# A hybrid decoder layer: the relative-bias product moved to the third value slice and done in one fp32r pass

## The chip, the cores and the metric

The kernel runs on one core of a Trainium2 chip. The metric is the device time of one execution in microseconds (us). Before the change the median of three runs is 200.31 us (199.53 to 201.07).

## The reference

One layer on x of 256 x 1024, float32. One projection `h = x @ w_in` gives queries, keys and values of two attention branches, their gates z, and two branch gates:

```python
ya = swa_sink_attention(qa, ka, va, sinks, table_a) * silu(za) @ w_out_a
yb = moba_attention(qb, kb, vb, table_b) * silu(zb) @ w_out_b
merged = sigmoid(ga + b_gate[:D]) * ya + sigmoid(gb + b_gate[D:]) * yb
x = layer_norm(alpha * x + merged @ w_out, gamma, beta)
```

Branch A has 8 query heads on 2 key heads, a window of 128 and one sink logit per head; branch B has 8 heads and, at 256 positions, one causal block. To the logits of every head a bias is added that depends on the distance of query and key: `rel_table[t5_bucket(distance), head]`, a table of 32 buckets by 16 heads.

## The kernel before, in words

**Numbers.** Most products are made of three fp32r products: an operand is split into a high part (rounded to fp32r by ScalarE, ACT) and the rest (a subtraction on VectorE, DVE), and high x high, high x low and low x high are summed. So each weight tile that SyncE (SP) loads is rounded by ACT (L138) and subtracted by DVE (L153) before TensorE (PE) uses it. The bias product (L312) is a plain fp32 product instead.

**Order.** The schedule is written by hand: each engine runs its instructions in the order of the program. `order` (L93 to L105) lists the weight pieces: eight value slices `v`, then the tiles `t` of keys, queries, gates, with the bias reads `r` put between them (one after each query tile), then `a`, `b` and `o`. `lead` (L167) runs `fetch` (load and rounding) some pieces ahead of the use and `split` (subtraction) one piece less ahead: at value slice k the fetch of slice k+2 and the split of slice k+1 are issued, and only then the products of slice k. A raw buffer serves five pieces (`RAWS`), so a load waits until the subtraction five pieces earlier is done.

**Value stage** (L302 to L318): for k = 0 to 7, twelve products of 320 columns each (L307) into four banks.

**Bias.** At k = 0 the value loop also makes, for two sets of heads, the product of the table with a one-hot matrix (L312), copies it reversed into `rvec` on DVE (L313) and writes `rvec` to the DRAM tensor `rd` by GpSimd (POOL) (L314). `fetch("r", n)` (L120) reads it back with a shifted row step, so that each partition gets its own diagonal: `toep`. SP's queue holds these reads in its fixed order: t0, t1, two reads of `rd`, t2, two reads, t3, and so on. The first read waits for the first write of `rd`. POOL also issues the small loads (L72 to L77: table, one-hot, sinks, gate bias), and after them builds the identity and `eps`.

**First projections.** `keys(KA, 0)` (L334) multiplies t0; in ACT's order the rounding of t2 comes before its copies of that product (L196). DVE (L198) and POOL (L200) then build `kall`; `queries` (L202) with t1 and t2 builds `q` (L206 to L212, POOL last). `scores` (L224 to L241) multiplies `q` by `kall`, adds `toep` (L226, L239) and takes exponentials. Twelve steps of this (L335) run through all heads, then gates, output and norm.

Of the kernel before, what the change touches and what calls it, by code (L numbers as in the profile page):

```python
# [11 lines left out]
F32 = mybir.dt.float32  # L12
F32R = mybir.dt.float32r
BF16 = mybir.dt.bfloat16
AF = mybir.ActivationFunctionType
ALU = mybir.AluOpType

P = 128
# [4 lines left out]
NB = 32  # L23
# [5 lines left out]
RL = 384  # L29
# [17 lines left out]
def hybrid_layer(ctx: ExitStack, tc: tile.TileContext, xT, x2, w_t, w_v, w_a, w_b, w_o,  # L47
                 b_gate, sinks, table, onehot, gamma, beta, out):
    nc = tc.nc
    const = ctx.enter_context(tc.tile_pool(name="const", bufs=1))  # L50
    wp = ctx.enter_context(tc.tile_pool(name="wp", bufs=1))
    work = ctx.enter_context(tc.tile_pool(name="work", bufs=2))
# [6 lines left out]
    def bank(tag):  # L59
        return psum.tile([P, 512], F32, tag=tag, name=f"ps_{tag}", bufs=banks[tag])  # L60
# [6 lines left out]

    rvec = work.tile([P, 2, RL], F32, tag="pr_", name="rvec", bufs=4)
    nc.gpsimd.memset(rvec, NEG)
    tab = const.tile([NB, 2 * P], F32, name="tab")  # L70
    oh = work.tile([NB, RL], F32, tag="res", name="oh")
    nc.gpsimd.dma_start(tab, table)  # L72
    nc.gpsimd.dma_start(oh, onehot)
    sink = const.tile([P, 8], F32, name="sink")
    nc.gpsimd.dma_start(sink, sinks)
    bg = const.tile([P, 16], F32, name="bg")
    nc.gpsimd.dma_start(bg, b_gate)  # L77
    ident = const.tile([P, P], F32, name="ident")
    make_identity(nc, ident)
    nsink = const.tile([P, 8], F32, name="nsink")  # L80
    eps = const.tile([P, 1], F32, name="eps")
    nc.gpsimd.memset(eps, LN_EPS)


    kall = const.tile([P, 3, 2, 2, S], F32R, tag="big12", name="kall")
# [87 lines left out]
    def weights(kind, n):  # L173
        lead(kind, n)
        return ready[kind, n]
# [126 lines left out]
    for k in range(NK):  # L302
        wh, wl = weights("v", k)
        for a, w, s0, s1 in ((xh, wh, k == 0, False), (xl, wh, False, False), (xh, wl, False, k == NK - 1)):
            for c in range(2):
                for t in range(2):
                    nc.tensor.matmul(vacc[t][c], a[:, k, t * P:(t + 1) * P], w[:, c * 320:(c + 1) * 320],  # L307
                                     start=s0, stop=s1)
        if k == 0:
            for s, (lo, hi) in enumerate(REACH):  # L310
                pr = bank("pt")[:, :hi - lo]
                nc.tensor.matmul(pr, tab[:, s * P:(s + 1) * P], oh[:, s * P:s * P + hi - lo], start=True, stop=True)  # L312
                nc.vector.tensor_copy(rvec[:, s, TOP + 1 - hi:TOP + 1 - lo], pr[:, ::-1])  # L313
                nc.gpsimd.dma_start(rd[s].rearrange("(p l) -> p l", p=P), rvec[:, s, :])  # L314
            nc.gpsimd.tensor_scalar_mul(nsink, sink, -1.0)
# [46 lines left out]
    for br, (tiles, w_y) in enumerate(((GA, "a"), (GB, "b"))):  # L362
        for c in range(8):
# [9 lines left out]
            else:  # L373
                m = work.tile([P, S], F32, name="m")
# [27 lines left out]
    for t in range(2):  # L402
        ts = slice(t * P, (t + 1) * P)
        res = work.tile([P, D], F32, tag="res", name="res")
# [129 lines left out]
```

## Time and profile before

| | us |
|---|---|
| median of 3 runs | 200.31 |
| the profiled execution | 199.98 |
| its span (first to last instruction) | 198.2 |
| PE busy in it | 189.4 |
| DVE, ACT, POOL busy | 135.5, 113.8, 47.8 |

PE is the TensorE matmul, PEld its weight loads. A group of instructions is named by its line in the kernel, its engine and "out<-in". "issue to landing" of a transfer counts from its issue until its data is there. Busy matmuls are pipelined, so each lasts longer than its distance to the next.

### The profile page before, as it was taken

The numbers are of one execution on the slowest core, as the hardware profiler recorded it, in microseconds if no ns is written. First come the engines' busy times: TensorE is split into PE (matmuls) and PEld (weight loads), VectorE is DVE, ScalarE is ACT, GpSimd is POOL, SyncE is SP. The second block draws the span as 40 slices with busy tenths as digits, with TensorE's granted clock in tenths as the row PEclk, the third lists the DMA queues.
The fourth block names the chain that finished last, engine by engine and source line by source line (L and its number), as shares of the span: only waits on it lengthen the run. The fifth ranks groups of instructions, "written<-read, shape, count | busy, mean of one in ns | idle before, by whom it ended". The sixth has DMA issues, their size and how long they took to land.

```text
span 198.2 us, 3922 instructions
## 1 busy us (share of the span) xinstructions
PE 189.4 (96%) x1469; PEld 177.9 (90%) x1469; DVE 135.5 (68%) x274; ACT 113.8 (57%) x228; POOL 47.8 (24%) x92
## 2 busy tenths in 40 slices
PE   8999999999999999999999999999999999999970
PEld 3799999799999999889999999999999999888860
DVE  0686277987797794586769537446685878785863
ACT  4675756578867867875669454245554746630211
POOL 7110083467699673020000000000000000003311
PEclk9999999999999999999999999999999999999998
DMA  5999999834453543054656885564847499300202
GB/s 131 300 401 364 286 322 302 264 121 159 136 187 109 174 146 111 0 160 161 211 173 203 314 246 157 185 212 140 286 146 244 158 342 341 154 0 0 106 0 106
DMA packets 14082, 37.43 MB, mean 189 GB/s; under 512 B 1632, under 2 KB 5744, under 8 KB 14064
## 3 DMA queue, kind: packets, MB, share of 16 engines
q1 hardware_dynamic: 13520, 36.51, 56.6%
q0 software_dynamic: 256, 0.49, 0.7%
q8 instruction: 11, 0.18, 0.4%
q10 hardware_dynamic: 288, 0.20, 0.3%
q14 instruction: 7, 0.06, 0.1%
HBM read 35.75 MB, written 1.44 MB: 188 GB/s over the span
## 4 chain that ended last, share of the span: by engine, by line
PE 73%; DMA 9%; DVE 5%; ACT 5%; POOL 3%; issue 2%; SPq 1%; DVEq 0%; ACTq 0%; POOLq 0%
PE ps_acc L181 18%; PE ps_acc L182 18%; PE ps_acc L184 18%; PE ps_acc L412 6%; DMA wraw<-in_w_v 5%; PE ps_sc L412 4%; DMA wraw<-in_w_t 3%; PE ps_pt L272 2%; PE ps_o L289 2%; PE ps_pt L412 1%; ACT wh L138 1%; PE ps_sc L232 1%; DVE wl L153 1%; PE ps_sc L224 1%; ACT pr__1159 L241 1%
## 5 line engine op out<-in xcount | busy, mean ns | idle before, releaser
L181 PE MATMUL ps_acc<-xh,wh 128*128 128x256 f32 x296 | 71.7, 281 | 0.0
L182 PE MATMUL ps_acc<-xl,wh 128*128 128x256 f32 x296 | 71.4, 280 | 0.0
L153 DVE TENSOR_TENSOR wl<-wraw,wh 128x1024 fp32r<-128x1024 f32 (+1 forms) x53 | 61.2, 1169 | 6.6 <-ACT wh L138 6.3
L138 ACT ACTIVATE wh<-wraw 128x1024 fp32r<-128x1024 f32 (+2 forms) x54 | 52.7, 989 | 8.4 <-DMA wraw<-in_w_v 4.1
L181 PEld LDWEIGHTS ps_acc<-xh,wh 128*128 128x128 f32 x296 | 55.8, 189 | 0.2 <-issue 0.2
L182 PEld LDWEIGHTS ps_acc<-xl,wh 128*128 128x128 f32 x296 | 55.8, 188 | 0.0
L184 PE MATMUL ps_acc<-xh,wl 128*128 128x256 f32 x296 | 40.9, 280 | 0.0
L184 PEld LDWEIGHTS ps_acc<-xh,wl 128*128 128x128 f32 x296 | 37.5, 189 | 0.0
L400 POOL CAST wh<-sums 128x2 fp32r<-128x2 f32 x8 | 1.4, 180 | 92.3 <-ACT sums L396 92.3
L367 ACT ACTIVATE sg<-ps_acc,bg 128x256 f32<-128x256 f32 x16 | 7.6, 474 | 19.1 <-PE ps_acc L184 19.1
L181 PE MATMUL ps_acc<-yh,wh 128*128 128x256 f32 x64 | 15.8, 281 | 0.0
L182 PE MATMUL ps_acc<-yl,wh 128*128 128x256 f32 x64 | 15.8, 280 | 0.0
L200 POOL CAST kall<-kall 64x512 fp32r<-64x512 f32 x10 | 10.7, 1066 | 15.0 <-DVE kall L198 14.5
L372 DVE TENSOR_TENSOR ga<-ps_acc,sg 128x256 f32<-128x256 f32 x8 | 3.4, 424 | 13.7 <-ACT wh L138 13.7
L181 PEld LDWEIGHTS ps_acc<-yh,wh 128*128 128x128 f32 x64 | 12.1, 188 | 0.0
L182 PEld LDWEIGHTS ps_acc<-yl,wh 128*128 128x128 f32 x64 | 12.0, 188 | 0.0
L184 PE MATMUL ps_acc<-yh,wl 128*128 128x256 f32 x64 | 10.1, 279 | 0.0
L377 ACT ACTIVATE mm<-m 128x256 fp32r<-128x256 f32 x8 | 3.3, 418 | 11.6 <-DVE m L376 11.6
L150 DVE TENSOR_TENSOR wl<-wraw,wh 128x1024 fp32r<-128x1024 f32 x8 | 9.7, 1218 | 0.1
L198 DVE TENSOR_TENSOR kall<-ps_acc,kall 64x256 fp32r<-64x256 f32 x10 | 4.2, 422 | 7.8 <-ACT kall L196 7.6
L412 PE MATMUL ps_acc<-wh,mm 128*128 128x512 f32 x32 | 8.8, 396 | 0.0
L184 PEld LDWEIGHTS ps_acc<-yh,wl 128*128 128x128 f32 x64 | 8.6, 188 | 0.0
(170 smaller groups left out, 306.5 us busy)
## 6 DMA issues: line engine op xcount, KB each, us to landing
wraw<-in_w_t SPq DMA_DIRECT2D x37, 512.0 KB, 4.1
wraw<-in_w_o SPq DMA_DIRECT2D x8, 512.0 KB, 4.9
wraw<-in_w_v SPq DMA_DIRECT2D x7, 320.0 KB, 5.4
toep<-rd SPq DMA_DIRECT2D x16, 128.0 KB, 6.5
wraw<-in_w_a SPq DMA_DIRECT2D x4, 512.0 KB, 3.2
wraw<-in_w_b SPq DMA_DIRECT2D x4, 512.0 KB, 3.9
xraw<-in_xT SPq DMA_DIRECT2D x8, 128.0 KB, 5.2
xr<-in_x SPq DMA_DIRECT2D x1, 1024.0 KB, 7.4
```

The costliest lines, as they stand in the source:

```text
L138: nc.scalar.activation(wh[:, cut], raw[:, cut], AF.Copy)
L150: nc.vector.tensor_sub(quarters(wl), raw.rearrange("p (a b) -> p a b", a=4), quarters(wh).bitcast(F32))
L153: nc.vector.tensor_sub(wl[:, :width], raw[:, :width], wh[:, :width].bitcast(F32))
L181: nc.tensor.matmul(acc, wh[:, cols[k]], ah[:, a0 + k, :], start=(k == 0), stop=False)
L182: nc.tensor.matmul(acc, wh[:, cols[k]], al[:, a0 + k, :], start=False, stop=False)
L184: nc.tensor.matmul(acc, wl[:, cols[k]], ah[:, a0 + k, :], start=False, stop=(k == n - 1))
L198: nc.vector.tensor_sub(l[r, j, :], acc[r, :], h[r, j, :].bitcast(F32))
L200: nc.gpsimd.tensor_copy(kall[halves[1 - j], b, :, j, :], kall[r, b, :, j, :])
L272: nc.tensor.transpose(pt[:, b * P:(b + 1) * P], pr[:, j, b * P:(b + 1) * P], ident)
L289: nc.tensor.matmul(o[r, :], vv[:, 0, c], pts[:, :S], start=True, stop=False)
L367: nc.scalar.activation(sg, acc, AF.Sigmoid, bias=bg[:, at:at + 1])
L412: nc.tensor.matmul(acc, a[:, k, ts], w[:, q:q + n, :cols], start=s0, stop=s1)
```

## The change

The small loads are issued after the identity and `eps`. The table and the one-hot are loaded twice each, on partitions 0 to 31 and 32 to 63, and POOL casts the one-hot to fp32r (`places`). At the end of k = 1 ACT rounds the table to fp32r on all 64 rows (`parts`), and DVE replaces the lower 32 rows by the rest. At the end of k = 2 one fp32r product over 64 rows takes the place of the fp32 product of k = 0; the copies and the writes to `rd` follow it there.

```diff
--- before.py
+++ after.py
@@ -67,19 +67,24 @@
 
     rvec = work.tile([P, 2, RL], F32, tag="pr_", name="rvec", bufs=4)
     nc.gpsimd.memset(rvec, NEG)
-    tab = const.tile([NB, 2 * P], F32, name="tab")
-    oh = work.tile([NB, RL], F32, tag="res", name="oh")
-    nc.gpsimd.dma_start(tab, table)
-    nc.gpsimd.dma_start(oh, onehot)
-    sink = const.tile([P, 8], F32, name="sink")
-    nc.gpsimd.dma_start(sink, sinks)
-    bg = const.tile([P, 16], F32, name="bg")
-    nc.gpsimd.dma_start(bg, b_gate)
     ident = const.tile([P, P], F32, name="ident")
     make_identity(nc, ident)
     nsink = const.tile([P, 8], F32, name="nsink")
     eps = const.tile([P, 1], F32, name="eps")
     nc.gpsimd.memset(eps, LN_EPS)
+
+    rows = [slice(i * NB, (i + 1) * NB) for i in range(2)]
+    tab = const.tile([2 * NB, 2 * P], F32, name="tab")
+    oh = work.tile([2 * NB, RL], F32, tag="res", name="oh")
+    for r in rows:
+        nc.gpsimd.dma_start(tab[r, :], table)
+        nc.gpsimd.dma_start(oh[r, :], onehot)
+    sink = const.tile([P, 8], F32, name="sink")
+    nc.gpsimd.dma_start(sink, sinks)
+    bg = const.tile([P, 16], F32, name="bg")
+    nc.gpsimd.dma_start(bg, b_gate)
+    places = work.tile([2 * NB, RL], F32R, tag="pts", name="places", bufs=4)
+    nc.gpsimd.tensor_copy(places, oh)
 
 
     kall = const.tile([P, 3, 2, 2, S], F32R, tag="big12", name="kall")
@@ -306,10 +311,14 @@
                 for t in range(2):
                     nc.tensor.matmul(vacc[t][c], a[:, k, t * P:(t + 1) * P], w[:, c * 320:(c + 1) * 320],
                                      start=s0, stop=s1)
-        if k == 0:
+        if k == 1:
+            parts = work.tile([2 * NB, 2 * P], F32R, tag="m", name="parts")
+            nc.scalar.activation(parts, tab, AF.Copy)
+            nc.vector.tensor_sub(parts[rows[1], :], tab[rows[1], :], parts[rows[1], :].bitcast(F32))
+        if k == 2:
             for s, (lo, hi) in enumerate(REACH):
                 pr = bank("pt")[:, :hi - lo]
-                nc.tensor.matmul(pr, tab[:, s * P:(s + 1) * P], oh[:, s * P:s * P + hi - lo], start=True, stop=True)
+                nc.tensor.matmul(pr, parts[:, s * P:(s + 1) * P], places[:, s * P:s * P + hi - lo], start=True, stop=True)
                 nc.vector.tensor_copy(rvec[:, s, TOP + 1 - hi:TOP + 1 - lo], pr[:, ::-1])
                 nc.gpsimd.dma_start(rd[s].rearrange("(p l) -> p l", p=P), rvec[:, s, :])
             nc.gpsimd.tensor_scalar_mul(nsink, sink, -1.0)
```

## Rows read from the trace of the kernel before

**Rows 1.** The page: busy time, and the granted clock in 40 slices.
```profile
PE 189.4 (96%) x1469; PEld 177.9 (90%) x1469; DVE 135.5 (68%) x274; ACT 113.8 (57%) x228; POOL 47.8 (24%) x92
...
PEclk9999999999999999999999999999999999999998
```

**Rows 2.** Waits of PE: line, who released it, us in total, times, longest.
```profile
PE ps_sc L224 <- POOL q L212: 0.5, 1, 0.5
PE ps_sc L224 <- DVE nm L239: 0.5, 1, 0.5
...
PE ps_pt L272 <- POOL pr__1159 L264: 0.4, 1, 0.4
```

**Rows 3.** The chain of waits, 16 to 31 us: start, us, what.
```profile
16.01 6.66 DMA wraw<-in_w_t
...
22.75 1.06 ACT wh L138
23.81 0.34 ACT kall L196
...
27.37 0.39 POOL q L211
...
27.83 1.28 POOL q L212
...
30.07 0.40 PE ps_sc L224
...
30.50 0.43 DVE low L226
```

**Rows 4.** Timeline of SP's queue, 11 to 17 us: start, us, instruction.
```profile
11.88 1.54 SPq L133 DMA_DIRECT2D wraw<-in_w_t  x2
14.67 1.25 SPq L120 DMA_DIRECT2D toep<-rd  x2
16.01 0.54 SPq L133 DMA_DIRECT2D wraw<-in_w_t  x1
```

**Rows 5.** Waits of SP's queue.
```profile
SPq L120 <- DMA rd<-rvec: 1.2, 1, 1.2
```

**Rows 6.** Timeline of PE: the bias product, and the first products of slices 1 and 3.
```profile
7.47 0.92 PE L312 MATMUL ps_pt<-oh,tab 32*128 32x128 f32 x4
...
8.31 0.19 PEld L307 LDWEIGHTS ps_acc<-wh,xh 128*128 128x128 f32 x1 [0.33 <-ACT xh L124]
...
11.80 0.19 PEld L307 LDWEIGHTS ps_acc<-wh,xh 128*128 128x128 f32 x1
```

**Rows 7.** Timeline of DVE, 8 to 12 us.
```profile
8.71 0.61 DVE L313 COPY rvec<-ps_pt 128x128 f32<-128x128 f32 x2
...
10.31 0.42 DVE L146 TENSOR_TENSOR xl<-xraw,xh 128x256 fp32r<-128x256 f32 x1
11.02 0.83 DVE L153 TENSOR_TENSOR wl<-wraw,wh 128x640 fp32r<-128x640 f32 x1 [0.29 <-ACT wh L138]
```

**Rows 8.** Timeline of ACT: the rounding of slices 1 and 3.
```profile
7.20 0.74 ACT L138 ACTIVATE wh<-wraw 128x640 fp32r<-128x640 f32 x1 [0.69 <-DMA wraw<-in_w_v]
...
10.25 0.74 ACT L138 ACTIVATE wh<-wraw 128x640 fp32r<-128x640 f32 x1 [0.43 <-DMA wraw<-in_w_v]
```

**Rows 9.** Timeline of POOL: its first load, the writes of the bias.
```profile
1.40 0.73 POOL L72 DMA_DIRECT2D tab<-in_table  x1
...
9.29 1.11 POOL L314 DMA_DIRECT2D rd<-rvec  x2 [4.93 <-DVE rvec L313]
```

**Rows 10.** DMA issues: count, KB, us to landing; the tile is the one issued at 33.91.
```profile
rd<-rvec POOLq DMA_DIRECT2D x2, 192.0 KB, 5.5
...
wraw<-in_w_t SPq DMA_DIRECT2D x1, 512.0 KB, 4.4
...
wraw<-in_w_a SPq DMA_DIRECT2D x4, 512.0 KB, 3.2
```

**Rows 11.** DMA queues, first 9 us: packets, MB, share of 16 engines' time.
```profile
q0 software_dynamic: 128, 0.09, 5.2%
```

## The prediction

> **What bounds the kernel now.** Read the page's busy shares first: TensorE (PE) is busy 96% of the span, its clock is full except at the very end [rows 1]. Then ask where PE waits at all: after the first slices it waits three times, 1.4 us together [rows 2]. So the kernel is a PE stream, and a change can pay only by taking work out of that stream or one of those waits, and can cost by making a wait longer. The longest two stand at the scores, L224; the chain of waits says what ends the first one, at 30.07 us [rows 3]: the third key/query weight tile (call it t2, the second query tile) is issued at 16.01, lands 6.66 us later, is rounded by ScalarE (ACT) at 22.75, and only then, because ACT works in order, ACT copies the key product (L196); VectorE (DVE) and GpSimd (POOL) build the key and query operands, and PE gets the second query half at 30.07. The third view is SyncE's queue (SP): t2's issue stands behind the first two toep reads, and these wait for the bias rows to land in DRAM [rows 4], 1.2 us already now [rows 5]. So the bias product, tiny on PE, is the head of a chain that ends in a PE wait. That is what the change moves.
>
> **The change part by part.** The sums are made against the profiled execution, 199.98 us (span 198.2 and 1.8 around it); the median of the three runs is 200.31, so 0.33 is added at the end.
>
> *The product leaves value slice k=0.* Now two fp32 products (four matmul records) run from 7.47, and the next slice starts behind them at 8.31 [rows 6]. Its weights were rounded by 7.20+0.74 = 7.94 [rows 8]. Without the product it can start at about 7.98: a gain of 0.33 us, not of the 0.84 us that the product takes, since the rest lay in a wait for ACT. DVE also loses 0.61 us of copies there [rows 7].
>
> *Small loads later, six for four.* The identity and eps go first; the first load issue moves from 1.40 to about 2.1. With at most 0.73 us each [rows 9] the second copy of the one-hot is issued by about 4.5; with the 5.5 us that the slower POOL transfers took [rows 10] it lands by 10.0. Nothing needs it before the new place of the product (11.4, below). I cost it at nothing; the cover is 1.4 us, less the cast that follows.
>
> *The cast of the one-hot on POOL (64x384).* Nearest are the 64x256 casts: 0.39 us in the open and 1.28 us beside a DVE subtraction [rows 3], so 0.6 to 1.9 for one and a half times the width. I take 0.6 to 1: done by about 11, just in time. At 1.9 it is done at 11.9, which is no later than the DVE step it is joined with. Skill sentence: "GPSIMD Engine Reference", Key points, in the Trainium skill, says that GpSimd shares its SBUF interfaces with VectorE and contends with two-input DVE instructions; the two durations just given agree, and by that rule the cast would come out near 1.9, by the open row near 0.6; the sum is the same either way.
>
> *Table parts (ACT copy 64x256, DVE subtraction 32x256) at k=1.* In ACT's order the copy comes after the rounding of slice 3's weights, which ends at 10.25+0.74 = 10.99 [rows 8]. The key copy on 64 partitions took 0.34 to its release [rows 3], so the copy ends at about 11.37. The DVE subtraction (0.42 as for 256 columns [rows 7]) is placed behind slice 2's and ahead of slice 3's, so it runs 11.41 to 11.8, and slice 3's xl and wl, which began at 10.31 and 11.02 [rows 7], follow it: xl to 12.1, wl to about 12.9.
>
> *The product at k=2.* Two slices take 11.80-8.31 = 3.49 us [rows 6]; from 7.98, PE is through slice 2 at 11.47, and waits for the parts until 11.85: +0.38. The new products are 384 columns; the bounds are 0.84 us (as the fp32 pair now) and, at the pace of the stream (slice: 12 products of 320 columns in 1.75 us), 384/320 x 0.146 = 0.18. I take 0.3, nearest to the stream's fp32r rows, as the short product may not run at the full pace. Slice 3 so starts at about 12.15 instead of 11.80: PE +0.35 net, the 0.33 gained at the front included. Slice 3's wl is wanted two thirds into the slice, at 13.3, and is there at 12.9: no further wait.
>
> *What goes on from there.* The two copies (L313) stand in DVE's order behind slice 3's wl: they start at about 12.85 instead of 8.71, and the first write to DRAM is issued 9.29-8.71 = 0.58 after that, at 13.4 instead of 9.29 [rows 7, 9]: +4.1 us. It lands 5.4 to 5.5 later [rows 10], about 18.8, against 14.67 now. SP's order is fixed: the two weight tiles t0 and t1 go out earlier (each a microsecond or so later than now, since their buffers come free with slice 3's and 4's wl; they are wanted after slice 7), then SP sits on the first toep read, and behind it wait t2, two more toep reads, t3 and so on. The two reads cost 1.34 us up to t2's issue [rows 4], so t2 is issued at about 20.15.
>
> *Its landing.* Now 6.66 us, into a full queue. After the hold SP has had nothing to issue for about 4 us, and the queue is nearly drained. Bounds: 3.2 us (the median of the branch weights, same size) and 6.66; the nearest row is a tile issued into a short queue, 4.4 us [rows 10]. So t2 lands at 24.5, 1.9 us later than now; and if the DRAM write, too, is a little faster in a thinner queue (5.1), 1.6 us later. I take 1.6. By the bounds it is 0.7 to 4.1. t3 follows t2 through the same queue at the same distance, so it sets nothing by itself.
>
> *What hides and what does not.* Every step between t2's landing and 30.07 is back to back [rows 3], so PE gets its operands at 31.7. PE itself comes to that point 0.35 later than now, so its wait grows from 0.5 by 1.6 less 0.35, to about 1.8 us, and all the small gains and losses on PE before it (0.33, 0.38, 0.3) vanish in it. After 30.07 PE is the bound again nearly without gaps [rows 2], and the first toep rows, read at 19 to 20, are not used before 30.5 [rows 3]: the 1.6 us stay. 199.98 + 1.6 + 0.33 = 201.9 us.
>
> **The rivals.** *Hidden after all.* If the DRAM write and t2 land as fast as the fastest rows (3.2 each), the first toep read goes at 16.6, t2 at 17.95, and it lands at 21.2, before 22.67: then the key copy waits for PE alone, 0.2 to 0.35 later: 200.5 us. For it: the queue is thinner. Against it: the writes took 5.5 us, and t0 and t1 are in flight with them.
>
> *Faster.* One mechanism: slice 1 starts 0.33 earlier, and the parts are ready early enough (no wait at 11.47), with the hold on SP so short that t2 is not late. Then the operands come at the old time or up to the 0.5 of the wait earlier, and the gain is at most 0.33+0.5 = 0.83: 199.5 us. It decides from t2's issue: at 16.0 or before. Against it: DVE's order alone puts the DRAM write 3 us or more later. A gain over 1% (2.0 us) is more than those three waits and the 0.33 hold (1.7), so it is all but excluded.
>
> *Worse.* The added loads delay the value weights of slice 3. The software queue's packets took 5.2% of all engines' time in the first 9 us [rows 11], 0.47 us; the doubled table and one-hot can add as much again. Slice 3's rounding, the parts, wl, the write and t2 then all come 0.3 to 0.5 later, and t2's landing is nearer to 6.66 than to 4.4, say 5.7, if the toep reads ahead of it fill the queue as they do now: 1.6 + 0.4 + 1.3 = 3.3: 203.6 us. Skill sentence: "DMA: Bandwidth & Descriptors", Issuing engines are not separate DMA queues, in the Trainium skill, says that transfers issued from GpSimd and SyncE run on the same 16 engines and interleave; by that rule the extra loads do slow the weights, and the share in rows 11 bears it out in kind. A clock that falls in a wait of nearly 2 us would be dearer still, but in rows 1 it falls only at the end, with PE idle.
>
> *Not what it says.* If the fp32r products are no quicker than the fp32 pair (0.84), PE comes to 30.07 another 0.5 late: still inside the wait, no change to the sum.
>
> **How the numbers follow.** Forecast (t2 late by 0.8 to 2.6 us: 201.1 to 202.9) 0.47; hidden 0.25; faster 0.10; worse 0.18. The range that leaves out most of the faster case and the far end of the worse one is 200.0 to 203.7. About 1% (2.0 us) is what a measurement here can tell from no change. Slower by over 1%: two fifths of the forecast case and nearly all of the worse one, 0.36. Faster by over 1%: 0.04. Within: 0.60.
>
> **What would show it.** Right: slice 1's first product near 8.0; a PE wait of about 0.4 ahead of L312 at k=2; the DRAM write issued near 13.4; SP waiting for it 4 us or more at L120 (1.2 now); t2 issued near 20; PE waiting over 1.5 us at L224. Wrong: t2 issued before 18, or a chain to the first scores that no longer runs through t2; or PE gaps of their own in slices 3 to 7.

## The result, and the profile after

The changed kernel takes 202.45 us (median of 4 runs, 202.35 to 203.16) against 200.49 for the kernel before in the same comparison: ratio 1.0112, 95% interval 1.0082 to 1.0142. It is slower by about 2 us, inside the range and on the side that was forecast (201.9). In the sections below "before" is 200.24 to 200.28 us, the medians of the larger comparisons that the experiments ran in. The profiled execution of the changed kernel took 203.16 us, span 201.4; its line numbers are five higher than before up to the value loop, and those of the kernels below differ by a few more.

The waits of PE in the changed kernel (line, who released it, us in total, times, longest):

```profile
PE ps_sc L229 <- POOL q L217: 1.6, 2, 1.1
PE ps_acc L312 <- ACT wh L143: 1.3, 1, 1.3
...
PE ps_pt L321 <- DVE parts L317: 0.4, 1, 0.4
```

The wait at the first scores was 0.5 [rows 2] and is now 1.6; the wait for the parts is new. The 1.3 at L312 is the gap ahead of value slice 1, which the fp32 product used to fill [rows 6].

The chain of waits of the changed kernel, 13 to 33 us (start, us, what), beside [rows 3]:

```profile
13.29 0.29 DVE rvec L322
...
13.87 4.76 DMA rd<-rvec
18.64 0.62 SPq L125
...
19.99 5.35 DMA wraw<-in_w_t
25.42 1.06 ACT wh L143
26.48 0.27 ACT kall L201
...
28.41 1.50 POOL kall L205
...
30.43 1.28 POOL q L217
...
32.68 0.57 PE ps_sc L229
```

The chain now starts at the bias copies and runs through the DRAM write and the first toep read into t2, as was forecast. t2 is rounded at 25.42 instead of 22.75, 2.67 us later, and the first scores' second half comes at 32.68 instead of 30.07, 2.61 later: nothing between the two gave.

What the small parts did stands in the timelines of the changed kernel (start, us, instruction, idle before it and who ended it), first PE:

```profile
8.16 0.42 PE L312 MATMUL ps_acc<-wh,xh 128*128 128x320 f32 x1 [1.28 <-ACT wh L143]
...
12.32 0.46 PE L321 MATMUL ps_pt<-places,parts 64*128 64x128 f32 x2 [0.38 <-DVE parts L317]
12.71 0.42 PE L312 MATMUL ps_acc<-wh,xh 128*128 128x320 f32 x1
```

then ACT:

```profile
7.37 0.74 ACT L143 ACTIVATE wh<-wraw 128x640 fp32r<-128x640 f32 x1 [1.16 <-DMA wraw<-in_w_v]
...
10.68 0.74 ACT L143 ACTIVATE wh<-wraw 128x640 fp32r<-128x640 f32 x1 [0.65 <-DMA wraw<-in_w_v]
11.33 0.40 ACT L316 ACTIVATE parts<-tab 64x256 fp32r<-64x256 f32 x1
```

DVE:

```profile
11.76 0.41 DVE L317 TENSOR_TENSOR parts<-tab,parts 32x256 fp32r<-32x256 f32 x1 [1.30 <-ACT parts L316]
...
12.55 0.82 DVE L158 TENSOR_TENSOR wl<-wraw,wh 128x640 fp32r<-128x640 f32 x1
13.29 0.61 DVE L322 COPY rvec<-ps_pt 128x128 f32<-128x128 f32 x2
```

POOL:

```profile
9.16 0.51 POOL L87 CAST places<-oh 64x384 fp32r<-64x384 f32 x1 [3.87 <-DMA oh<-in_onehot]
13.87 1.08 POOL L323 DMA_DIRECT2D rd<-rvec  x2 [4.20 <-DVE rvec L322]
```

and SP's queue:

```profile
13.43 1.89 SPq L138 DMA_DIRECT2D wraw<-in_w_t  x2
18.64 1.25 SPq L125 DMA_DIRECT2D toep<-rd  x2
19.99 0.94 SPq L138 DMA_DIRECT2D wraw<-in_w_t  x1
```

Slice 1 starts at 8.16 (8.31 before): little is gained, because its weights were rounded only by 7.37+0.74 = 8.11. The cast is done at 9.67, far ahead of the parts, so the parts alone set the product: 0.38 us of waiting, then 12.71-12.32 = 0.39 for the two fp32r products. Slice 3's first product is at 12.71. In the kernel before it was at 11.94, 0.77 us earlier; the 11.80 in [rows 6] is the load of its weights, which runs ahead of it:

```profile
11.94 0.31 PE L307 MATMUL ps_acc<-wh,xh 128*128 128x320 f32 x1
```

One thing more is in this execution. Its busy shares by microsecond (us, PE busy, PEld, DVE, ACT, POOL, granted clock, DMA share, GB/s):

```profile
31.00:32.00 1.00, 0.24 (x1) 0.19 (x1) 0.44 (x1) 0.76 (x1) 0.94 (x2) 1.00 0.98 315
32.00:33.00 1.00, 0.46 (x2) 0.32 (x2) 0.40 (x1) 0.57 (x2) 0.88 (x3) 0.86 1.03 410
33.00:34.00 1.00, 1.00 (x6) 1.00 (x6) 0.59 (x3) 0.00 (x0) 0.88 (x3) 0.50 1.11 293
...
37.00:38.00 1.00, 1.00 (x11) 1.00 (x10) 0.80 (x1) 1.00 (x2) 0.00 (x0) 1.00 1.03 301
```

After the two waits PE ran at 0.50 of full speed, the 1.2 GHz level, for some 3 us (0.50 in each of the three from 33 to 36): 6 products in a full us, against 11 once the clock is back at 2.4 GHz. "TensorE: Matmul & The Clock Gate", Part 1, in the Trainium skill, says that the clock has these two levels and follows how busy the array has lately been; these rows agree.

### The profile page after: what moved, and what is told of

Read it like the earlier page. It is cut to its first block, busy times and chain, and to the rows that moved or that the text cites. A ratio compares the mean times of both kernels' runs of the same rounds, so it can differ in the third digit from the quotient of the medians.

```text
span 201.4 us, 3923 instructions
## 1 busy us (share of the span) xinstructions
PE 190.5 (95%) x1467; PEld 179.6 (89%) x1467; DVE 135.6 (67%) x275; ACT 113.9 (57%) x229; POOL 49.3 (25%) x95
## 4 chain that ended last, share of the span: by engine, by line
PE 76%; DMA 8%; DVE 3%; ACT 3%; POOL 3%; SPq 2%; issue 2%; DVEq 0%; ACTq 0%; POOLq 0%
PE ps_acc L186 19%; PE ps_acc L187 19%; PE ps_acc L189 19%; PE ps_acc L421 6%; PE ps_sc L421 4%; DMA wraw<-in_w_v 3%; PE ps_pt L277 3%; DMA wraw<-in_w_t 3%; DMA rd<-rvec 2%; PE ps_sc L237 2%; PE ps_o L294 2%; PE ps_pt L421 1%; PE ps_sc L229 1%; ACT pr__1166 L246 1%; POOL kall L205 1%
## 5 line engine op out<-in xcount | busy, mean ns | idle before, releaser
L186 PE MATMUL ps_acc<-xh,wh 128*128 128x256 f32 x296 | 72.8, 284 | 0.0
L187 PE MATMUL ps_acc<-xl,wh 128*128 128x256 f32 x296 | 72.4, 283 | 0.0
L186 PEld LDWEIGHTS ps_acc<-xh,wh 128*128 128x128 f32 x296 | 56.7, 191 | 0.2 <-issue 0.2
L187 PEld LDWEIGHTS ps_acc<-xl,wh 128*128 128x128 f32 x296 | 56.5, 191 | 0.0
```

Of the source, the lines that this page charges most:

```text
L186: nc.tensor.matmul(acc, wh[:, cols[k]], ah[:, a0 + k, :], start=(k == 0), stop=False)
L187: nc.tensor.matmul(acc, wh[:, cols[k]], al[:, a0 + k, :], start=False, stop=False)
```

## The experiments

The theory to test, called the hold: the late DRAM write holds SP's queue, t2 comes late behind it, and PE waits at the first scores. Its rival, called the front: the time is lost in the value stage, to loads, parts and product.

**The move alone.** The kernel before with only the place of the product changed:

```diff
-        if k == 0:
+        if k == 2:
             for s, (lo, hi) in enumerate(REACH):
```

> The kernel before, with the fp32 bias product, its copies and writes moved from k=0 to k=2 and nothing else. Theory of the hold (the late DRAM write holds SyncE's queue, so t2 comes late and TensorE waits at the first scores): the copies stand behind slice 3's subtraction, about 11.8, the write goes out about 12.3 (9.29 before, 13.87 after), t2 is issued about 18.7 (16.01 and 19.99), the first scores come about 1.5 us later than before: 201.5 to 202.0 us. Rival (the front: the loss is what TensorE loses in the value stage to loads, parts and product): the product of 0.84 us now stands in the dense stream and 0.33 is gained at k=0, 0.5 in all: 200.9 to 201.1 us.

Measured: 200.87 us, ratio 1.0046 (1.0023 to 1.0069). The hold's 201.5 to 202.0 failed. SP does wait for the write (first read at 16.92, write at 12.96, t2 at 18.27), but t2 then landed in 4.2 us instead of 6.66, so it is rounded no later than before (22.58, and 22.75 before), and in ACT's timeline the key copy waits for PE, not for t2's rounding:

```profile
22.58 1.09 ACT L138 ACTIVATE wh<-wraw 128x1024 fp32r<-128x1024 f32 x1
24.56 0.78 ACT L196 ACTIVATE kall<-ps_acc 64x256 fp32r<-64x256 f32 x2 [0.89 <-PE ps_acc L184]
```

So with PE 0.8 us later, a t2 issued at 18.27 and landing in 4.2 us has no cost of its own. The 0.6 us are the rival's: the fp32 product of 0.84 us now stands in the dense stream, and the first scores come 0.81 later (30.88). The rival's 200.9 to 201.1 is missed by 0.03.

**The loads alone.** The kernel before with its four small loads moved behind the constants:

```diff
-    nc.gpsimd.dma_start(tab, table)
...
     nc.gpsimd.memset(eps, LN_EPS)
+    nc.gpsimd.dma_start(tab, table)
```

> The kernel before, with its four small loads issued after the identity and eps; product at k=0. Hold theory: the one-hot lands by about 7.5, just when the product starts (7.47), so the write moves by 0.3 us at most, and t2 with it: 200.3 to 200.8 us. Rival (the later small loads slow the value weights): slice 1's weights land 0.2 later as in the changed kernel and TensorE keeps that loss: 200.7 to 201.0 us, with t2's issue unmoved.

Measured: 200.43 us, ratio 1.0000 (0.9979 to 1.0021); t2's issue at 16.01, as before. Later loads cost nothing that this interval can tell.

**The reads one tile later.** This is the deciding run: the changed kernel, with t2 ahead of the first reads in SP's order.

```diff
+    held = []
     for t in range(GA):
-        order += [("t", t)]
+        order += [("t", t)] + held
+        held = []
         if QA <= t < KQB:
-            order.append(("r", t - QA))
+            held = [("r", t - QA)]
...
```

> The changed kernel, with each pair of toep reads put one weight tile later in SyncE's order, so that t2 goes ahead of the first reads. Hold theory: t2 is issued when its buffer comes free, about 16 (19.99 in the changed kernel), lands by 21.5, the key copy waits for TensorE alone (its key tile ends about 24.5), the first scores come about 30.8 to 31.2, the clock stays up, 200.6 to 201.3 us: half or more of the loss is gone though the bias and the loads stay where the change put them. Rival (the front): nothing of this matters, 202.2 to 202.6 us.

Measured: 201.00 us, ratio 1.0041 (1.0021 to 1.0060). With the bias, loads and parts where the change put them, 202.45-201.00 = 1.45 us of the loss are gone (1.4 by the two ratios, each to the kernel before in its own comparison). Its SP queue, with t2 the third of the tiles at the first row:

```profile
13.73 2.96 SPq L140 DMA_DIRECT2D wraw<-in_w_t  x3
17.97 1.26 SPq L127 DMA_DIRECT2D toep<-rd  x2
```

and its key copy is released by PE:

```profile
24.97 0.78 ACT L203 ACTIVATE kall<-ps_acc 64x256 fp32r<-64x256 f32 x2 [0.92 <-PE ps_acc L191]
```

The 201.00-200.24 = 0.76 us above the kernel before that stay are the front's.

**The control**, the same shift in the kernel before:

> The kernel before with the same shift of the reads, the control. Hold theory: t2 is issued about 14.4 instead of 16.01, but the key tile ends at 23.62 and the key copy starts at 23.77 already, so at most 0.2 us: 200.1 to 200.5 us. If the shift by itself were worth a microsecond or more (its own effect, not the hold's), 199.0 to 199.5 us.

Measured: 200.07 us, ratio 0.9992 (0.9976 to 1.0007). By itself the shift is worth 0.2 us by the medians, and nothing that the interval can tell, so the 1.45 us, or all but 0.2 of them, are the hold's.

**A larger dose.** The changed kernel with parts at k=2 and product at k=3:

```diff
-        if k == 1:
+        if k == 2:
             parts = work.tile([2 * NB, 2 * P], F32R, tag="m", name="parts")
...
-        if k == 2:
+        if k == 3:
             for s, (lo, hi) in enumerate(REACH):
```

> The changed kernel with everything of the bias one slice later: parts at k=2, product, copies and writes at k=3; SyncE's order as in the changed kernel. Theory of the hold: the parts are ready when the product comes, so TensorE loses no 0.38 us there, but the write goes out about 1.0 to 1.7 us later than 13.87, t2 is issued about 21 to 21.7, and the first scores come 1 us or more after 32.68: 203.0 to 204.5 us. Rival (the front): without the wait for the parts TensorE gains 0.4: 201.9 to 202.2 us.

Measured: 203.83 us, ratio 1.0188 (1.0151 to 1.0225). PE no longer waits for parts, yet the kernel is slower still, as the hold says and the front denies. SP's queue, PE at the first scores, and the chain of waits ahead of them:

```profile
19.81 1.45 SPq L125 DMA_DIRECT2D toep<-rd  x2
21.36 0.54 SPq L138 DMA_DIRECT2D wraw<-in_w_t  x1
```

```profile
33.24 0.38 PE L229 MATMUL ps_sc<-kall,q 128*128 128x256 f32 x1 [1.86 <-POOL q L217]
34.16 0.38 PE L229 MATMUL ps_sc<-kall,q 128*128 128x256 f32 x1 [0.54 <-POOL q L217]
```

```profile
23.21 6.58 DMA wraw<-in_w_t
...
29.87 1.06 ACT wh L143
```

The tile in this chain is not t2 but t3, which stands behind the next two reads in the same queue: its rounding comes ahead of the query copy in ACT's order. So here t3 sets the first scores, which the prediction had left out ("it sets nothing by itself").

**Both**, product at k=3 and the reads one tile later:

> The same, with the reads one tile later in SyncE's order as in the third run. Hold theory: t2 is ahead of the hold, so what is left is the front alone; with the parts ready, TensorE pays the product (0.39) and what slice 1's weights come late: 200.4 to 200.9 us, less than the 201.00 of the product at k=2 with the reads later. If the write's delay still counted by another way (t3 behind the reads, or the bias late for the scores), 201.5 us or more.

Measured: 201.26 us, ratio 1.0053 (1.0033 to 1.0073). The write is the latest of all (15.77) and costs nothing more that the intervals can tell (201.00 had 1.0021 to 1.0060), so the bias itself is not late for the scores. But it is not better than the 201.00 with the product at k=2, as the wait for the parts that it avoids should have made it: that part of the expectation failed. In its profiled execution slice 1 began only at 9.34, for weights that landed late.

**What the front is made of.** Two runs more on the 0.76 us: the changed kernel with the reads later and all six loads ahead of the constants, and the kernel before with the reads later and the six loads, the second copies unused.

```diff
     nc.gpsimd.memset(rvec, NEG)
-    ident = const.tile([P, P], F32, name="ident")
-    make_identity(nc, ident)
...
     nc.gpsimd.dma_start(bg, b_gate)
+    ident = const.tile([P, P], F32, name="ident")
+    make_identity(nc, ident)
...
```

> The changed kernel with the reads one tile later (third run) and its six small loads issued ahead of the constants again. It splits the 0.8 us that the third run left, the front. If the place of the loads is part of the front (slice 1 starts late because the value weights land late), slice 1 starts at 8.0 to 8.2 and the time is 200.4 to 200.8 us; if the front is the wait for the parts and the product in the stream (0.2 to 0.4 and 0.39), nothing moves: 200.9 to 201.2 us.

Measured: 201.10 us, ratio 1.0035 (1.0012 to 1.0058).

```diff
-    nc.gpsimd.dma_start(tab, table)
-    nc.gpsimd.dma_start(oh, onehot)
...
+    for r in rows:
+        nc.gpsimd.dma_start(tab[r, :], table)
+        nc.gpsimd.dma_start(oh[r, :], onehot)
...
```

> The kernel before with the reads one tile later, and of the change the loads alone: table and one-hot loaded twice, all six loads after the constants; the fp32 product at k=0 uses the first copy, the second is read by nothing. If the doubled loads delay the value weights by the 0.3 to 0.5 us that the software queue's share allows, 200.4 to 200.7 us; if they hide, as 200.07 of the same kernel with four loads: 200.0 to 200.2 us.

Measured: 200.30 us, ratio 1.0005 (0.9983 to 1.0026). The place of the loads is not the front. For their number the run falls between its two expectations: 0.23 us above the same kernel with four loads (200.07), which the two intervals cannot tell from nothing; that a part of the 0.76 is theirs is neither shown nor excluded. Seen in the traces are the product in the stream (0.39 us in the changed kernel) and the wait for the parts (0.38). How the 0.76 divides is not settled, since the run without that wait (product at k=3) was no faster.

**The clock.** Four products of constants on PE ahead of the first scores, their result unused:

```diff
+        if i == 1:
+            warm = bank("o")
+            for _ in range(4):
+                nc.tensor.matmul(warm, nc.const_aps.tensor(1.0, [P, P], BF16), ...)
```

> The changed kernel with four products of constants (128x512, bf16) on TensorE just ahead of the first scores, where it waited 1.06 us; their result is not used. If the waits of 1.06 and 0.54 us are what let the clock fall after 32.8 us, it stays at 2.4 GHz, and the time is 0.3 to 1 us less than the changed kernel's: 201.4 to 202.1 us. If the fall costs nothing in the median, or is not due to the wait: 202.3 to 202.7 us.

Measured: 202.32 us, ratio 1.0115 (1.0073 to 1.0157), no change. The waits shrank to 0.34 and 0.54 and the clock stayed up in the profiled execution, but in it the operands also came earlier (second half at 32.09, against 32.68; the tile that set them was t3, as with the product at k=3), so it does not isolate the clock. And the changed kernel once more:

> The changed kernel itself, timed in the same call as its variants: 202.2 to 202.7 us. The look at the trace is for the clock: if the fall after the first scores belongs to every execution it is there again; if it depends on how long the waits happen to be, t2's landing differs with it.

Measured: 202.67 us, ratio 1.0113 (1.0072 to 1.0153). Here the waits were 0.92 and 0.54, and the clock stayed up: 202.56 us in the profiled execution. So the fall belongs to some executions: the 203.16 of the first profile holds it, the 202.56 of the second does not, and as the medians (202.45 and 202.67) lie near the second, the 2 us do not need it.

**A version that beats both?** With t2 free of the hold, DVE can subtract it, and t3, while it is idle, ahead of the key parts and not beside POOL's casts. First t2 alone, then both, in the kernel before with the reads later (shown for both; for t2 alone the step is taken at ("t", 0) only):

```diff
-        advance(1, at, far - 1)
+        advance(1, at, far - ((kind, n) not in (("t", 0), ("t", 1))))
```

> The kernel before with the reads one tile later and with VectorE's subtraction for t2 issued ahead of the key parts, while VectorE is idle, so that it no longer runs beside GpSimd's key casts. If the second key cast's 1.50 us (0.6 in the open) is due to that subtraction, GpSimd is done about 0.9 us sooner, TensorE's wait of 0.53 at the first scores goes, and the time is 199.5 to 199.8 us, below both kernels. If the cast is slow for another reason, nothing moves: 200.0 to 200.3 us.

Measured, t2 alone: 199.92 us, ratio 1.0001 (0.9979 to 1.0023), short of the gain that was expected: the key casts are fast now, but the query cast runs beside t3's subtraction. POOL's key and query casts:

```profile
25.27 1.28 POOL L202 CAST kall<-kall 64x512 fp32r<-64x512 f32 x2 [13.97 <-DVE kall L200]
...
27.69 1.33 POOL L214 CAST q<-ql 64x256 fp32r<-64x256 f32 x1
```

> The kernel before with the reads one tile later and VectorE's subtractions for both t2 and t3 issued one step earlier. In the run with t2's alone the wait at the first scores went from 0.53 to 0.32 us, and the first query cast on GpSimd still took 1.33 beside t3's subtraction. With both earlier the cast runs in the open, one key cast is slowed instead, GpSimd is done by about 29.3 and the wait goes: 199.4 to 199.8 us, below both kernels. If the key cast loses what the query cast gains, 199.9 to 200.1 us.

Measured, both: 199.77 us, ratio 0.9976 (0.9950 to 1.0001). The same casts:

```profile
25.23 2.22 POOL L202 CAST kall<-kall 64x512 fp32r<-64x512 f32 x2 [14.73 <-DVE kall L200]
...
27.97 0.40 POOL L214 CAST q<-ql 64x256 fp32r<-64x256 f32 x1
```

The slow cast follows the subtraction: the two key casts take 1.28 us together in the open and 2.22 beside one, the query cast 0.40 and 1.33. "GPSIMD Engine Reference", Key points, in the Trainium skill, says that the two engines contend for SBUF when DVE reads two inputs; these rows agree. PE's wait at the first scores is gone (both halves from 29.34 on), but its next wait, at the third scores, grew from 0.45 to 0.69: they come at 38.20, only 0.18 us earlier than with the reads later alone (38.38). The medians differ by 0.5 us from the kernel before and by 0.3 from that run (200.07), and the interval of the ratio still touches 1: a gain of a few tenths is likely, not shown.

## Why the prediction was right

One table carries it, from the profiled execution of each kernel (us from the span's start) and the medians:

| kernel | DRAM write issued | first read issued | t2 issued | first scores, second half | median |
|---|---|---|---|---|---|
| before | 9.29 | 14.67 | 16.01 | 30.07 | 200.24 |
| before, reads later | 9.60 | 14.82 | before the reads | 30.05 | 200.07 |
| loads alone | 9.53 | 14.66 | 16.01 | 30.17 | 200.43 |
| move alone | 12.96 | 16.92 | 18.27 | 30.88 | 200.87 |
| changed, reads later | 14.16 | 17.97 | before the reads | 31.26 | 201.00 |
| changed | 13.87 | 18.64 | 19.99 | 32.68 | 202.45 |
| changed, second profile | 14.14 | 17.84 | 19.20 | 32.43 | 202.67 |
| product at k=3 | 14.80 | 19.81 | 21.36 | 34.16 | 203.83 |
| product at k=3, reads later | 15.77 | 20.59 | before the reads | 31.71 | 201.26 |

Where t2 stands behind the reads, the time follows the write; where it stands ahead of them, it does not. The mechanism was right. That the sum comes as near as it does is partly luck, as the terms show.

*Slice 1 near 8.0:* 8.16, and from 8.01 to 9.34 in the other profiles with the product moved. The 0.33 us were counted on where the weights landed in the one profile of before; that differs by some tenths or more from execution to execution. This gain was not there. The sum also took 3.49 us for two slices from the weight loads in [rows 6]; from first product to first product they take 11.94-8.32 = 3.62.

*Wait for the parts 0.38, product 0.3:* measured 0.38 and 0.39. The fp32r product costs less than half of the fp32 pair, and more than the stream's pace.

*The cast, 0.6 to 1 us and done by about 11:* 0.51, done at 9.67. (At the 1.9 us of the upper bound it would have been done 0.1 us after the DVE step, not "no later".)

*The write at 13.4:* 13.87. Slice 3's weights were rounded at 11.42 and not at 10.99, and everything behind them on ACT and DVE moved with it.

*SP holding 4 us or more:* 3.2 (1.2 before). t1 went out only at 15, later than the step allowed for. The hold's end, which counts, came at 18.64, as forecast (18.5 to 18.8).

*t2 issued at 20.15:* 19.99. *Its landing, 4.4 us:* 5.35. This is the term that was mis-sized, and not because the queue was fuller than in the row that was taken. That row was not a short queue, as the sum called it: around its issue the DMA engines' share was 1.01 and 0.81 (33 to 35 us, the kernel before). In the changed kernel it was 0.24 from 19 to 20 us, when t2 was issued, and 0.53 to 0.71 in the three us after. With the product at k=3 it was 0.00 from 20 to 21, and t2, issued at 21.36, still took 4.7. After the hold t2 landed in 4.2 (move alone) to 5.9 us (second profile of the changed kernel); why is open. The sum of the errors is the difference: 1.6 + 0.47 (write) - 0.34 (its landing, 4.76 against 5.1) + 0.95 = 2.7 us, as t2's 2.67 late. In the second profile the same sum has other terms: the write 0.74 later than forecast, its landing 3.70 us, t2's 5.9, t2 rounded 2.43 us late. Errors of 1 us and more cancel there, and this is the luck.

*All of the front vanishes in the wait:* so it does in the changed kernel, but the front is larger than the 0.35 us of the sum: 0.76 us with the hold taken away. It lies under the hold, so taking the hold away gives back 1.45 and not all of the 2.67 by which t2 is late.

*After 30 us the loss stays:* yes. In the second profile of the changed kernel the first scores are 2.36 us late and the execution 202.56-199.98 = 2.58.

The rivals: "hidden" needed t2 issued before 18, and it was 19.99; the move alone shows that this rival was near, for at 18.27 the hold is hidden. "Worse" was right that t2's landing is longer than 4.4, but its cause, the added loads slowing the value weights by 0.3 to 0.5 us, is not shown (200.30 with all six loads, 200.07 with four). "Faster" had nothing for it. That the clock falls only at the end holds for the kernel before [rows 1]; in one profile of the changed kernel it fell after waits of 1.06 and 0.54 us close together, in another, with 0.92 and 0.54, it did not.

## What to carry to other kernels

A product of under a microsecond can be the head of the longest chain: before moving it, follow what reads its result, and look above all at the in-order queue in which that reader waits, for everything behind it in that queue moves too. Here putting the next weight tile ahead of the waiting reads gave back 1.45 of 2 us without touching the product. And work that fills a gap in the bound engine's stream is nearly free there; moved into the dense part it costs its length: the fp32 product of 0.84 us, moved alone, put the first scores 0.81 us later.

## What the runs showed that was not expected

The granted clock fell to 0.50 for about 3 us after two PE waits of 1.6 us in all in the first profile of the changed kernel; with the product at k=3 (waits of 1.86 and 0.54, and 0.8 more just before) it fell again to 0.50. The profiled execution of the changed kernel with the fall took 203.16 us, the one without it 202.56. At the first scores the one with the fall was 0.25 us behind the other, at the second 37.73-35.95 = 1.78, at the fourth 49.88-49.27 = 0.61: three quarters of what the slow stretch lost was made up around the third scores, where PE waits without the fall (0.44 us ahead of them) and not with it.

POOL's cast of 64x256 took 0.40 us or 1.33 by nothing but the place of a DVE subtraction, so moving the subtractions of t2 and t3 by one step of the schedule takes 0.9 us out of POOL's chain; a DVE wait further on kept most of it from the total.
